# Two kinds of attention heads in turns, head by head, on one Trainium2 core

## Chip, cores and metric

The kernel runs on one core of one Trainium2 chip. The metric is the device time of one execution in microseconds (us); lower is better. Three runs of the kernel before took 2731.16, 2734.02 and 2737.94 us, a median of 2734.02 us.

## The reference, cut to what matters

One layer of an encoder for 2048 tokens of width 1024, all in float32: an adaLN-modulated RMS norm, a mixer with 16 heads of width 64, an output projection with a residual, a second norm, and a squared-ReLU MLP of width 4096. Eight heads are stick-breaking attention (called SB here) over all earlier keys:

```python
z = jnp.einsum('bqhd,bkhd->bhqk', qb, kb).astype(jnp.float32) * scale
log_beta = jax.nn.log_sigmoid(z)
log_1m_beta = jnp.where(strict, jax.nn.log_sigmoid(-z), 0.0)
suffix = lax.cumsum(log_1m_beta, axis=3, reverse=True) - log_1m_beta
w = jnp.where(strict, jnp.exp(log_beta + suffix), 0.0)
outs.append(jnp.einsum('bhqk,bkhd->bqhd', w.astype(v.dtype), vb))
```

The other eight are softmax attention over the query's own chunk of 64 keys and the eight chunks before it, with a learned bias (called CA here):

```python
s = jnp.einsum('bnqhd,bnkhd->bnhqk', qc, k_band).astype(jnp.float32) * (d ** -0.5)
s = s + bias[None, None]
p = jax.nn.softmax(s, axis=-1)
out = jnp.einsum('bnhqk,bnkhd->bnqhd', p.astype(v.dtype), v_band)
```

The heads' outputs stand side by side, SB first, and go through the output projection together. No head needs another head's result.

## The kernel before, in words

The program has three stages. The first makes the adaLN columns, the first norm and most of the input projection. The second, from about 457 us to 1408 us, is the attention. The third is the output projection of the last group of tokens and the MLP; it is almost all matrix products.

Tokens stand in reversed order, so "earlier keys" have higher indices, in four groups g of 512 tokens. Each float32 product is made of products of high and low halves in a reduced format; that is why operands come in pairs (`wth` and `wtl`, made by `split`: ScalarE copies the high part, VectorE subtracts to get the low part).

The attention's work is a list of **units** (L926 to L929), taken in order. An SB unit is one head, one group g of queries and one block c of 512 keys, c from g to 3; a CA unit is one head and one group of queries with its whole band of up to 1024 keys. There are 80 SB units (8, 16, 24 and 32 in groups 3, 2, 1, 0) and 32 CA units. Each unit is four **steps** of 128 queries. In the loop over steps (L992) the step at the front computes scores and weights, and the step LAG = 8 behind it (two units) turns its weights round and multiplies them with the values. In the program's order one pass does this:

```python
for j in js:
    back.transposes(j)      # PE, into PSUM tile wt
if front is not None:
    front.soft1(fs)         # SB: ACT sigmoids, DVE scan, POOL product; CA: DVE sum and minimum
while first:
    first.pop(0)()          # CA, the step before: DVE reciprocal, POOL product
for j in js:
    back.parts(j)           # ACT wth, DVE wtl
if front is not None:
    front.soft2(fs)         # CA: ACT Exp
...
if i + 1 < len(steps):
    u, st = steps[i + 1]
    u.scores(st)            # PE, into PSUM tile z or cz
fill(front.weight if front else 0.6)
```

`Ordered` (L42) keeps TensorE (PE), ScalarE (ACT), VectorE (DVE) and GpSimd (POOL) in exactly this order, so nearly every instruction of the stage has line L42 in the profile and is told apart by its tile. An SB step (`soft1`, L680) has two Sigmoid activations, tiles `b` and `z`; a CA step (`soft2`, L770) has one Exp activation, tile `e`. Sigmoid and Exp are in different function tables of ScalarE: where one follows the other, the compiled program holds an ACT_TABLE_LOAD.

The tiles `z`, `cz`, `ct` and `wt` share four PSUM buffers (`ppz`, L554). A step of an SB unit takes two of them, `z` for its scores and `wt` for one block of its transposes; a step whose back is a CA unit of groups 0 to 2 takes two `wt`, as such a unit has eight blocks in four steps.

Loads of a unit (q, k, and the bias of CA, L560 to L576 and L716) are issued by SP two units ahead, its values (L578) two steps into the unit. SP works its DMA queue in order. The bias has two buffers, CA's values two, most others three.

`fill` (L938) puts matrix products of other work between the steps, so that PE always has something: the rest of the input projection (`pf`) and the output projection of finished groups (`po`). How much it puts into a step goes by the step's weight (1.0 for SB, 0.7 on the diagonal, 0.9 or 0.495 for CA) over the weight that is left; what does not fit is done at the end.

When a unit closes a head, `finish` (L587) folds the sums into half of a tile `o`; two heads share one `o`. `keep` (L599) then splits it into `os` (one buffer) and stores it.

Of the kernel before, what the change touches and what calls it, by code (L numbers as in the profile page):

```python
# [9 lines left out]
F32 = mybir.dt.float32  # L10
# [8 lines left out]
P = 128  # L19
# [3 lines left out]
NH = 8  # L23
DFF = 4096
KT = D // P
TB = 512
NTB = S // TB
# [40 lines left out]
def encoder_kernel(ctx, tc, xT, c, g1, g2, w_in, gqk, bias, w_o, w1, w2, w_ada, b_ada, out):  # L68
# [472 lines left out]
    with ExitStack() as ph:  # L541
# [6 lines left out]
        op = ph.enter_context(tc.tile_pool(name="op", bufs=2))  # L548
# [38 lines left out]
        def finish(u):  # L587
            r = (u.h % 2) * HD
            q = HD - r
            if u.h % 2 == 0:  # L590
                pend["o"] = op.tile([P, TB], F32, tag="o", name=f"o{u.nm}")
            o = pend["o"]
            tmp = op.tile([P, TB], F32, tag="otmp", name=f"otmp{u.nm}")
            act.copy(tmp[r : r + HD, :], u.acc[q : q + HD, :])
            dve.tensor_tensor(o[r : r + HD, :], u.acc[r : r + HD, :], tmp[r : r + HD, :], op=ALU.add)
            if u.h % 2:
                soon.append(lambda: keep(u, o))

        def keep(u, o):  # L599

            os = op.tile([P, 2, TB], F32R, tag="os", name=f"os{u.nm}", bufs=1)
            split(os[:, 0, :], os[:, 1, :], o, pool)
            sp.dma_start(scr_m[u.g, u.ca * 4 + u.h // 2], os.bitcast(F32))
            if u.ca and u.h == NH - 1 and u.g > 0:
                filler.append(Filler(outproj, u.g))

        pend = {}

        class Unit:
# [26 lines left out]
            def values(self, j):  # L636
                if j == 0 and self.first:
                    pend["acc"] = ppo.tile([P, TB], F32, tag="acc", name=f"acc{self.nm}")
                self.acc = pend["acc"]
                wh, wl, cols, kb = self.wt.pop(j)  # L640
                end = self.last and j == len(self.blocks) - 1
                pe.matmul(self.acc[:, cols], self.v[:, kb, :], wh[:, cols], start=self.first and j == 0, stop=False)
                pe.matmul(self.acc[:, cols], self.v[:, kb, :], wl[:, cols], start=False, stop=end)
                if end:
                    soon.append(lambda: finish(self))
# [279 lines left out]
        CAP = 5  # L925
        units = []  # L926
        for g in range(NTB - 1, -1, -1):
            units += [SB(h, g, c) for h in range(NH) for c in range(g, NTB)]
            units += [CA(h, g) for h in range(NH)]  # L929
        have = set()  # L930
        filler = [Filler(fill_qkv, 1, hts[1], (2, 3, 0, 1, 10, 11)), Filler(fill_qkv, 0, None, (2, 3, 0, 1, 4, 5, 10, 11))]
        work = 14 * 48.0 + 5 * KT * KT * 3 / 2
# [59 lines left out]
        for i in range(len(steps) + LAG):  # L992
# [29 lines left out]
            if i + 1 < len(steps):  # L1022
                u, st = steps[i + 1]
# [398 lines left out]
```

## Time and profile before

| | us |
|---|---|
| median of three runs | 2734.02 |
| the profiled execution | 2737.44 |
| its span, first to last instruction | 2735.7 |
| PE busy in the span | 2625.1 (96%) |
| VectorE busy | 1929.8 (71%) |
| ScalarE busy | 1528.5 (56%) |
| GpSimd busy | 1023.8 (37%) |

The span is cut into 40 slices of 68 us; slices 7 to 20, counted from 0, hold the attention. A busy digit is a share in tenths. The PE's busy time includes matrix products that are pipelined and whose ends are modelled. Idle time of an engine is put down to the semaphore that came last, written "<-" with the engine and tile that released it.

### The profile page before, as it was taken

How to read it: one execution, taken by the hardware profiler on the slowest of the kernel's cores; microseconds unless marked ns; L12 is line 12 of the kernel's file. 1: busy time of each engine (PE TensorE's matmuls, PEld its weight loads, DVE VectorE, ACT ScalarE, POOL GpSimd, SP SyncE). 2: the span in 40 equal slices, each digit the busy share in tenths (PEclk: the TensorE clock that was granted, in tenths of full speed). 3: DMA queues.
4: the chain of work that ended last, by engine and by line, in shares of the span. 5: the costliest groups of instructions: out<-in, count | busy, mean ns of one | idle time of the engine just before them, and what ended most of it. 6: DMA issues, size and time to landing. Idle time of an engine off the chain costs nothing.

```text
span 2735.7 us, 42897 instructions
## 1 busy us (share of the span) xinstructions
PE 2625.1 (96%) x14192; PEld 2235.5 (82%) x14192; DVE 1929.8 (71%) x3329; ACT 1528.5 (56%) x2926; POOL 1023.8 (37%) x1116
## 2 busy tenths in 40 slices
PE   6998999899999999999988999999999999999999
PEld 5898998678778987878876888888878888888887
DVE  7565575788789988989747887765597655555564
ACT  5422433788678878878634455454465454544443
POOL 5342454566466656767524332100022422100000
PEclk9999999999999999999998999999999999999999
DMA  8978885987888688766777887785576444555574
GB/s 327 337 273 320 288 295 190 275 261 240 276 245 257 199 249 272 231 212 194 205 252 272 280 284 256 271 298 191 191 254 243 158 148 148 177 197 199 189 258 142
DMA packets 311197, 653.52 MB, mean 239 GB/s; under 512 B 29376, under 2 KB 118464, under 8 KB 301888
## 3 DMA queue, kind: packets, MB, share of 16 engines
q1 hardware_dynamic: 310336, 649.22, 70.7%
q8 instruction: 112, 1.84, 0.3%
q10 hardware_dynamic: 640, 1.57, 0.2%
q14 instruction: 109, 0.89, 0.1%
HBM read 459.31 MB, written 191.37 MB: 238 GB/s over the span
## 4 chain that ended last, share of the span: by engine, by line
PE 52%; DVE 2%; DMA 1%; ACT 1%; issue 1%; POOL 0%; SPq 0%; DVEq 0%; ACTq 0%
PE ps L42 44%; PE po L42 3%; PE acc L42 2%; PE wt L42 2%; PE z L42 1%; DVE h L129 1%; DVE ty L1063 1%; PE cz L42 0%; DMA wo<-scr_wo 0%; DMA ty<-scr_x 0%; DMA out_dram<-tx 0%; DVE tx L1301 0%; DVE p L42 0%; POOL ty L1106 0%; ACT ty L1107 0%
## 5 line engine op out<-in xcount | busy, mean ns | idle before, releaser
L42 PE MATMUL ps<-h,opw 128*128 128x512 f32 x2688 | 613.4, 391 | 6.7 <-ACT opw L128 4.0
L42 PE MATMUL ps<-oph,opv 128*128 128x512 f32 x2688 | 614.9, 391 | 4.1 <-DVE opv L129 3.5
L42 PEld LDWEIGHTS ps<-h,opw 128*128 128x128 f32 x2688 | 506.6, 189 | 113.3 <-ACT opw L128 4.5
L42 PEld LDWEIGHTS ps<-oph,opv 128*128 128x128 f32 x2688 | 506.4, 189 | 110.8 <-DVE opv L129 4.2
L42 POOL TENSOR_TENSOR b<-b,p 128x512 f32<-128x512 f32 (+1 forms) x320 | 359.6, 1124 | 197.0 <-DVE p L42 174.9
L42 DVE TENSOR_TENSOR wtl<-wt,wth 128x512 fp32r<-128x512 f32 (+3 forms) x544 | 290.4, 545 | 49.7 <-ACT wth L42 47.2
L42 ACT CAST wth<-wt 128x512 fp32r<-128x512 f32 (+3 forms) x544 | 257.5, 484 | 116.0 <-PE wt L42 99.9
L42 PE MATMUL pt<-wh,ht 128*128 128x256 f32 x1664 | 307.4, 286 | 7.9 <-DVE ht L129 5.8
L129 DVE TENSOR_TENSOR oph<-hr,oph 128x512 fp32r<-128x512 f32 x224 | 156.0, 697 | 208.0 <-ACT oph L128 207.8
L128 ACT CAST oph<-hr 128x512 fp32r<-128x512 f32 x224 | 139.4, 622 | 291.4 <-PE ps L42 286.4
L42 PEld LDWEIGHTS pt<-wh,ht 128*128 128x128 f32 x1664 | 263.1, 193 | 9.1 <-DVE ht L129 6.2
L42 DVE TENSOR_TENSOR_SCAN p<-z,p,zero 128x512 f32<-128x512 f32 x192 | 246.0, 1281 | 33.6 <-ACT z L42 28.7
L42 PE MATMUL pt<-wl,ht 128*128 128x256 f32 x832 | 236.5, 284 | 0.0
L42 PE MATMUL acc<-wth,v 128*128 128x512 f32 (+3 forms) x544 | 221.7, 412 | 3.1 <-DMA v<-scr_v 3.1
L42 ACT ACTIVATE b<-z 128x512 f32<-128x512 f32 (+1 forms) x320 | 171.4, 536 | 66.7 <-PE z L42 50.7
L42 PE MATMUL z<-k,q 128*128 128x512 f32 (+3 forms) x640 | 187.7, 375 | 14.0 <-DVE p L42 5.9
L42 POOL TENSOR_TENSOR e<-e,cols 128x640 f32<-128x640 f32 (+4 forms) x128 | 143.0, 1120 | 147.5 <-DVE cols L42 81.6
L42 PE MATMUL acc<-wtl,v 128*128 128x512 f32 (+3 forms) x544 | 186.3, 349 | 0.0
L42 PE MATMUL wt<-ident,b 128*128 128x128 f32 x1088 | 172.5, 274 | 6.6 <-DVE cols L42 4.9
L42 ACT ACTIVATE z<-z 128x512 f32<-128x512 f32 (+1 forms) x320 | 170.6, 533 | 0.0
L42 PEld LDWEIGHTS wt<-ident,b 128*128 128x128 f32 x1088 | 133.9, 141 | 37.5 <-DVE cols L42 6.9
L42 PE MATMUL po<-fx,ow 128*128 128x512 f32 x576 | 162.5, 397 | 0.0
(207 smaller groups left out, 4536.7 us busy)
## 6 DMA issues: line engine op xcount, KB each, us to landing
hr<-scr_hid SPq DMA_DIRECT2D x112, 512.0 KB, 3.5
v<-scr_v SPq DMA_DIRECT2D x136, 256.0 KB, 4.3
k<-scr_k SPq DMA_DIRECT2D x268, 128.0 KB, 4.1
w<-in_w_dram SPq DMA_DIRECT2D x64, 512.0 KB, 4.2
wr<-scr_s SPq DMA_DIRECT2D x64, 512.0 KB, 4.1
q<-scr_q SPq DMA_DIRECT2D x124, 256.0 KB, 5.3
fw<-scr_w SPq DMA_DIRECT2D x28, 1024.0 KB, 6.4
wa<-in_w_ada_dram SPq DMA_DIRECT2D x48, 512.0 KB, 6.4
```

Source lines behind the costliest of these rows:

```text
L42: return lambda *x, **y: self.tc.keep_in_program_order(f(*x, **y))
L128: act.copy(hi, src)
L129: (lo_eng or dve).tensor_tensor(lo, src, hi.bitcast(F32), op=ALU.subtract)
L1063: eng.tensor_tensor(out, a, b, op=op)
```

## The change

```diff
@@ finish
             if u.h % 2 == 0:
-                pend["o"] = op.tile([P, TB], F32, tag="o", name=f"o{u.nm}")
-            o = pend["o"]
+                pend["o", u.ca] = op.tile([P, TB], F32, tag="o", name=f"o{u.nm}", bufs=3)
+            o = pend["o", u.ca]
@@ the list of units
         for g in range(NTB - 1, -1, -1):
-            units += [SB(h, g, c) for h in range(NH) for c in range(g, NTB)]
-            units += [CA(h, g) for h in range(NH)]
+            for h in range(NH):
+                units += [SB(h, g, c) for c in range(g, NTB)]
+                units.append(CA(h, g))
```

Within a group the order was SB head 0 to 7, then CA head 0 to 7. Now SB head 0 is followed by CA head 0, then SB head 1, CA head 1, and so on. As two heads of each kind are now open at once, each kind has a tile `o` of its own, and `o` has three buffers and not two. All units, their steps and their matrix products stay the same in kind and number.

## The prediction, as put on record

> **What bounds the kernel now.** I read the page's busy times, its slices and the first line of its chain.
>
> ```profile
> PE 2625.1 (96%) x14192; PEld 2235.5 (82%) x14192; DVE 1929.8 (71%) x3329; ACT 1528.5 (56%) x2926; POOL 1023.8 (37%) x1116
> ...
> ACT  5422433788678878878634455454465454544443
> ...
> PE 52%; DVE 2%; DMA 1%; ACT 1%; issue 1%; POOL 0%; SPq 0%; DVEq 0%; ACTq 0%
> ```
>
> PE is busy 96% of the span and is by far the largest part of the chain. So an edit that leaves the matrix products as they are can only move PE's waits. ScalarE's 56% hides that its digits are 6 to 8 in the attention (slices 7 to 20); elsewhere it idles.
>
> Next the busy time by stretch. In each group the first row is the SB part and the second the CA part.
>
> ```profile
> 457.00:507.00 50.00, 48.54 (x265) 37.74 (x266) 37.53 (x62) 37.43 (x96) 32.32 (x61) 0.90 0.83 237
> 507.00:565.00 58.00, 46.29 (x261) 37.46 (x259) 38.14 (x139) 40.20 (x112) 28.93 (x40) 0.94 0.91 261
> 565.00:685.00 120.00, 116.22 (x756) 100.66 (x755) 105.89 (x146) 100.45 (x214) 82.77 (x134) 1.00 0.81 249
> 685.00:772.00 87.00, 79.99 (x463) 67.27 (x462) 62.29 (x220) 56.80 (x130) 42.81 (x36) 0.94 0.86 268
> 772.00:965.00 193.00, 189.39 (x1194) 163.39 (x1194) 171.23 (x226) 158.31 (x328) 129.82 (x197) 0.99 0.75 233
> 965.00:1046.00 81.00, 78.45 (x514) 69.15 (x513) 64.24 (x223) 57.36 (x132) 42.95 (x36) 1.00 0.87 265
> 1046.00:1305.00 259.00, 252.58 (x1407) 206.78 (x1405) 233.75 (x304) 213.09 (x426) 192.33 (x275) 1.00 0.70 221
> 1305.00:1408.00 103.00, 99.18 (x599) 84.26 (x598) 77.86 (x258) 66.64 (x152) 50.32 (x42) 1.00 0.67 201
> ```
>
> The columns after the length are PE, weight load, DVE, ACT and POOL busy, granted clock, DMA share and GB/s. Over the eight rows PE is busy 910.6 of 951 us. It is idle 40.4 us here, and that is nearly all that mixing the heads could win. Two CA parts stand out, those of groups 3 and 2: idle 11.7 of 58 us and 7.0 of 87, both at clock 0.94. The two later CA parts are idle 2.6 of 81 and 3.8 of 103. In the SB parts DVE is close behind PE (233.75 of 259.00, 90%) and ACT not far (82%).
>
> **What the change removes.** The CA parts end as such, and with them the rush of their loads. The waits of PE and of SP's queue in the attention:
>
> ```profile
> PE cz L42 <- DMA k<-scr_k: 4.7, 4, 1.8
> PE pf L42 <- DMA fw<-scr_w: 4.5, 2, 2.9
> PE acc L42 <- DMA v<-scr_v: 3.1, 1, 3.1
> ...
> SPq L721 <- DVE cols L42: 27.8, 17, 3.3
> ```
>
> PE waits 12.3 us for these loads, and SP's queue stands 27.8 us, with all later loads behind it, until one of the two bias buffers is free. With one or more SB units between two CA units the bias and value buffers are long free when they are wanted. If the parts of groups 3 and 2 idled only like the CA part of group 1 (2.55 of 81 us, 3.1%), that gave 11.7 + 7.0 - 0.031 x 145 = 14.2 us; a full clock over the same 145 us gave 6% of it, 8.7 us. So at most 22.9 us. I take half, **11 us**: loads' bytes stay the same, the DMA share of group 3 is 0.83 and 0.91 in its two parts, so the mean does not fall, and the refilling of the input projection (`fw`) meets some heads' loads in either order. Bounds 0 and 22.9.
>
> **What it adds: table loads.** Before, ScalarE goes from Sigmoid to Exp once in each group and back once, except at the end. Now it does so for each head. The compiled order of ScalarE's instructions shows 64 table loads in place of 8; the rest has the same kinds and numbers.
>
> ```profile
> L42 ACT ACT_TABLE_LOAD x7 | 9.0, 1283 | 1.2 <-PE z L42 0.7 <-DVE cols L42 0.4
> ```
>
> One load takes 1283 ns, so 56 more are 71.8 us of ScalarE, 14 loads or 18 us in each group. ScalarE's busy time then is 95.6 of 108 us in group 3 (77.63 + 18 by the rows above) and 297.7 of 362 in group 0: 89% and 82%. It does not become the bound by throughput. What counts is where a load stands in the order. The 1.2 us of idle time ahead of the seven, released by `z` and `cols`, says that a load waits for the data of the activation behind it, so it mostly comes after the data and not ahead of them.
>
> **SB to CA.** Three switches of before, with what PE waited behind them:
>
> ```profile
> 687.20 1.28 ACT L42 ACT_TABLE_LOAD   x1
> 688.49 0.83 ACT L42 ACTIVATE e<-s,cols 128x640 f32<-128x640 f32 x1
> 690.42 0.73 PE L42 MATMUL cz<-k,q 128*128 128x512 f32 x2 [0.34 <-DVE wtl L42]
> ...
> 971.64 0.73 PE L42 MATMUL cz<-k,q 128*128 128x512 f32 x2 [0.48 <-DVE wtl L42]
> ...
> 1309.41 0.66 PE L42 MATMUL wt<-ident,b 128*128 128x128 f32 x4 [0.55 <-DVE cols L42]
> ...
> 1310.76 0.73 PE L42 MATMUL cz<-k,q 128*128 128x512 f32 x2 [0.23 <-DVE wtl L42]
> ```
>
> Behind the load in ScalarE's queue stand `e` and then the next `wth`; DVE's `wtl` waits for that, and PE waits for the PSUM buffer that `wtl` frees. Price: 0.34, 0.48 and 0.78 us, mean 0.53. The weights `e` themselves are wanted eight steps later, which hides them. I take **0.5 us** for each of 28 more: 14 us.
>
> **CA to SB.** Here the load stands ahead of both sigmoids, and the scan of DVE, which frees `z`, behind them.
>
> ```profile
> 569.17 0.50 PE L42 MATMUL z<-k,q 128*128 128x256 f32 x2 [1.20 <-DVE cols L42]
> ...
> 779.08 1.08 PE L42 MATMUL wt<-ident,e 128*128 128x128 f32 x5 [2.74 <-DVE cols L42]
> ...
> 1046.16 0.68 PE L42 MATMUL z<-k,q 128*128 128x512 f32 x2
> 1048.18 1.28 ACT L42 ACT_TABLE_LOAD   x1
> 1049.48 0.60 ACT L42 ACTIVATE b<-z 128x512 f32<-128x512 f32 x1
> 1050.59 1.22 DVE L42 TENSOR_TENSOR_SCAN p<-z,zero 128x512 f32<-128x512 f32 x1 [2.84 <-ACT z L42]
> 1051.87 1.08 PE L42 MATMUL wt<-ident,e 128*128 128x128 f32 x5 [1.81 <-DVE cols L42]
> ```
>
> The scores lay ready from about 1046.9 us; ScalarE finished the last `e`, loaded for 1.28 us, did both sigmoids, DVE scanned until 1051.81, and at 1051.87 PE had its buffer. PE stood 1.20, 2.74 and 1.81 us at the three switches. In the two longer cases a CA unit of eight blocks was at the back: two `wt` and one `z` a step use four buffers up after a step and a third. In the new order the unit two places behind the first SB unit of a head is the SB unit ahead of the CA unit (in group 3 too, where every unit takes one `wt` a step), so PE can do one more round of transposes and value products before it stops, 1.1 us by the rows at 1309.41 and 1310.76 (1310.76 - 0.23 - 1309.41). That makes 1.81 - 1.1 = 0.7, and the case that already has one `wt` a step, at 569.17, shows 1.2. I take **1.0 us**, nearest to those two: 28 us for 28 more.
>
> The Trainium skill speaks against this change: "ScalarE: Activation LUTs", section "Rules for kernel authors", has functions grouped by table set, all of one done before the switch. Its section "What ACT_TABLE_LOAD costs" gives 1283 ns, as the trace does, and a drain of 1380 ns more; the trace shows no drain, as `e` starts at 688.49, when the load that began at 687.20 ends.
>
> **What it moves.** CA's values now go to PE while SB units are at the front, and the reverse; the sums of each engine stay. In the SB parts PE idles 1.5 + 3.8 + 3.6 + 6.4 = 15.3 us, mostly for a DVE that is 90% busy; with CA in between, DVE's share is even (233.75 + 77.86 of 362 us, 86%). That can win some of it back. I take nothing, as SB units still follow each other in groups 0 to 2 and the new stalls eat DVE's slack too; bounds 0 and 8 us.
>
> **What costs nothing, and its cover.** The `os` tile has one buffer, and now two `os` follow one unit apart.
>
> ```profile
> scr_m<-os SPq DMA_DIRECT2D x32, 512.0 KB, 3.2
> PE z L42 <- DVE st L198: 5.4, 1, 5.4
> ```
>
> A store lands in 3.2 us; with the split ahead of it that still fits in a unit of 58/8 = 7 us, the shortest. Were it late, ScalarE would wait in four pairs of group 3, up to 4 us in all. The second row is the start of the stage: PE waits 5.4 us for the last tiles of the stage before. The first CA unit's k tile is now loaded there, in a buffer that overlaps those tiles; it is wanted four steps later, which hides it, and without that cover it costs up to another 5 us. The fill's weights sum to the same, so the work left for the end does not change, and the end of the list is the same CA unit.
>
> **Sum.** 14 + 28 - 11 = +31 us. Against the profiled execution's own 2737.4 us that is 2768; the median of the three runs is 2734.0, 3.4 us lower, so I say **2765 us**.
>
> **The rivals.**
>
> *A, the smoothing wins (faster).* The loads fall into time in which ScalarE waits anyway:
>
> ```profile
> ACT wth L42 <- PE wt L42: 99.9, 146, 7.0
> ```
>
> That is 99.9 us of waiting for PE ahead of this one tile, against 71.8 of loads. If ScalarE reaches a load 1.28 us ahead of its data, the load is free. The deciding point: at a switch ScalarE must have been idle that long before, and the load must not wait for its data. Then only 0.3 us a pair is left, 28 x 0.3 = 8, against the full 22.9: 2734 - 15 = 2719 us. For it: the idle parts of groups 3 and 2. Against it: PE waits behind all six switches shown, and the loads wait for data.
>
> *B, switches cost what they did.* 28 x (0.53 + 1.92) = 69 us, with 1.92 the mean of 1.20, 2.74 and 1.81. And the longest of these waits also cost clock:
>
> ```profile
> 778.00:782.00 4.00, 2.82 (x14) 2.25 (x15) 3.91 (x7) 2.90 (x8) 2.75 (x4) 0.85 0.98 296
> 782.00:786.00 4.00, 4.00 (x22) 3.47 (x20) 2.66 (x5) 2.08 (x7) 1.86 (x4) 0.73 0.74 198
> ```
>
> 0.15 x 4 + 0.27 x 4 = 1.7 us of clock; at one switch in three that is 16 us more. With 69, 16 and no more than 5 won, 2734 + 80 = 2814 us. For it: it is the plain mean of rows. Against it: two of its three rows had the eight-block unit at the back.
>
> *C, both small.* The loads are half hidden (about 15 us) and the smoothing gives 15: 2734 us, within 0.3%, which is 8 us and about what a measurement of this kernel can tell from no change.
>
> *D, a switch takes twice the row's load.* Then ScalarE has 144 us more, 36 in group 3 (113.6 of 108 us: it becomes the bound), and each switch is 1.28 us dearer: 2765 + 28 x 2 x 1.28 = 2837 us. The skill's drain, in "What ACT_TABLE_LOAD costs", would make it so; the row at 688.49 speaks against it.
>
> That the heads do not alternate is no rival: the compiled order of each engine shows them in turns.
>
> **How the numbers follow.** The forecast, with its own range 2743 to 2790, has a chance of 0.55; A 0.13; B 0.20; C 0.09; D 0.03. Faster by over 0.3%: 0.13 (A). Within: 0.09 (C). Slower: 0.78. The range reaches into A and to B's sum, **2720 to 2815**, and leaves out D, the better half of A and the worse tail of B, some 0.15.
>
> **What the profile of after would show.** 64 table loads of about 1.28 us and ScalarE at about 1600 us busy. Right: PE's idle time in the attention some 70 us, in waits of 0.3 to 1.5 us for `wtl`, `p` and `cols` just behind loads; waits for `scr_k`, `scr_v`, `scr_w` well under 12.3 us, and SP's wait for the bias gone. Wrong if PE hardly waits behind loads (A), if waits near 2 us with dips of clock follow most returns to SB (B), or if the loss sits in the first and last 20 us of the stage.

## The result, and the profile after

| | before | after |
|---|---|---|
| median, five runs of each (us) | 2737.31 (2731.16 to 2738.68) | 2803.60 (2800.86 to 2804.67) |
| ratio, 95% interval | | 1.0238 (1.0224 to 1.0252) |
| the profiled execution | 2737.44 | 2804.67 |

The change costs 66.3 us. The direction is that of the forecast and the time lies in its range, but the loss is more than twice the 31 us of the sum.

First two of the same lines of the page, now of after: the busy times and ScalarE's slices.

```profile
PE 2641.4 (94%) x14192; PEld 2239.1 (80%) x14192; DVE 1928.9 (69%) x3329; ACT 1592.3 (57%) x2982; POOL 1026.4 (37%) x1116
...
ACT  5423433887878877878862444554455445544443
```

The matrix products are the same 14192. ScalarE is busy 1592.3 us against 1528.5, with 56 more instructions, and its slices 7 to 19 stand at 7 and 8 throughout, slice 20 at 6. The loads themselves, from the costliest groups:

```profile
L42 ACT ACT_TABLE_LOAD x64 | 82.1, 1283 | 4.0 <-DVE cols L42 2.5 <-PEq L1411 0.7
```

64 of them, 1283 ns each as before.

Next the busy time by group. The boundaries are the first score product of each group and, at the end, of the last CA unit, so that both fences cover nearly the same work (that of after has 24 matrix products more); the columns are those of the windows above. Before:

```profile
457.20:564.60 107.40, 94.45 (x522) 74.92 (x523) 75.28 (x199) 77.51 (x208) 60.85 (x99) 0.92 0.87 249
564.60:771.90 207.30, 196.49 (x1217) 168.11 (x1217) 168.42 (x365) 157.28 (x345) 125.97 (x169) 0.98 0.83 257
771.90:1046.20 274.30, 268.14 (x1710) 232.84 (x1709) 235.67 (x448) 215.98 (x460) 172.77 (x232) 0.99 0.79 243
1046.20:1379.60 333.40, 323.21 (x1833) 266.65 (x1831) 292.19 (x509) 261.72 (x538) 231.35 (x307) 1.00 0.70 219
457.20:1379.60 922.40, 882.29 (x5276) 742.52 (x5276) 771.56 (x1520) 712.48 (x1547) 590.95 (x806) 0.98 0.78 238
```

After:

```profile
461.10:583.60 122.50, 95.86 (x523) 76.46 (x524) 75.97 (x196) 93.88 (x217) 59.29 (x98) 0.91 0.76 222
583.60:809.90 226.30, 203.76 (x1230) 173.18 (x1229) 170.00 (x376) 175.75 (x368) 125.78 (x170) 0.97 0.81 246
809.90:1100.00 290.10, 269.72 (x1711) 231.75 (x1710) 234.74 (x451) 232.18 (x475) 173.20 (x233) 1.00 0.74 229
1100.00:1451.30 351.30, 330.83 (x1842) 268.02 (x1841) 292.04 (x511) 278.30 (x557) 233.61 (x310) 0.99 0.66 205
461.10:1451.30 990.20, 900.17 (x5300) 749.42 (x5301) 772.75 (x1532) 780.11 (x1614) 591.88 (x808) 0.98 0.73 223
```

Each group is longer by about as much: 15.1, 19.0, 15.8 and 17.9 us, 67.8 in all. A group has 8 heads and so 14 loads more, whatever its length; a loss that goes with the number of switches and not with the work looks like this. PE's idle time rises from 40.1 (922.40 - 882.29) to 90.0 us; the other 17.9 us are busy time. The 24 products are some of it; but over the whole program, with the same 14192 products, PE is busy 16.3 us longer (2641.4 against 2625.1). The stage also begins 3.9 us later.

The waits of the attention, after, with the total, the times and the longest:

```profile
ACT wth L42 <- PE wt L42: 115.2, 129, 6.0
...
PE z L42 <- DVE cols L42: 45.5, 31, 3.1
...
PE cz L42 <- DVE wtl L42: 9.1, 13, 1.3
...
PE cz L42 <- DMA k<-scr_k: 5.9, 1, 5.9
```

There are 31 returns from CA to SB, and 30 of them show a wait of the third score product `z` for `cols`, the reciprocal that DVE makes just behind the scan: 44.8 us of the 45.5, 1.49 us each. (The 31st wait of the row, 0.75 us, stands ahead of a first score product.) The way to CA shows in 13 waits for `wtl`, at most 1.3 us. ScalarE still idles 115.2 us for PE ahead of `wth`, so it has time for the loads, only not at the places where they stand. One return in the timeline of after (group 0), the lines of PE, ScalarE and DVE that matter:

```profile
1143.50 0.63 PE L42 MATMUL z<-k,q 128*128 128x512 f32 x2
1143.77 0.83 ACT L42 ACTIVATE e<-s,cols 128x640 f32<-128x640 f32 x1
...
1144.01 0.94 PE L42 MATMUL po<-fx,ow 128*128 128x512 f32 x3
...
1144.70 1.28 ACT L42 ACT_TABLE_LOAD   x1
...
1145.99 0.60 ACT L42 ACTIVATE b<-z 128x512 f32<-128x512 f32 x1
...
1147.17 1.23 DVE L42 TENSOR_TENSOR_SCAN p<-z,zero 128x512 f32<-128x512 f32 x1 [2.57 <-ACT z L42]
...
1148.45 0.50 PE L42 MATMUL z<-k,q 128*128 128x256 f32 x2 [1.27 <-DVE cols L42]
```

PE has the scores ready at 1144.1; then the load, two sigmoids and the scan pass one after the other, and at the third `z` PE stands 1.27 us. That is the place the prediction named. The returns are not alike: the 16 behind CA units of groups 3 and 2 stop PE for 1.91 us on average, the 15 behind those of groups 1 and 0 for 0.94. At 15 of the 16 a copy `otmp` of 0.58 us, part of closing a head, stands on ScalarE ahead of the load; at the 15 others it does not.

### The profile page after: what moved, and what is told of

It reads as the page before. It is cut to its first block, busy times and chain, and to the rows that moved or that the text cites. A ratio compares the mean times of both kernels' runs of the same rounds, so it can differ in the third digit from the quotient of the medians.

```text
span 2802.8 us, 42713 instructions
## 1 busy us (share of the span) xinstructions
PE 2641.4 (94%) x14192; PEld 2239.1 (80%) x14192; DVE 1928.9 (69%) x3329; ACT 1592.3 (57%) x2982; POOL 1026.4 (37%) x1116
## 3 DMA queue, kind: packets, MB, share of 16 engines
q8 instruction: 112, 1.84, 0.3%
## 4 chain that ended last, share of the span: by engine, by line
PE 42%; DVE 4%; DMA 2%; issue 1%; POOL 1%; ACT 1%; SPq 0%; DVEq 0%; POOLq 0%; ACTq 0%
PE ps L42 39%; PE po L42 1%; DVE h L129 1%; DMA ty<-scr_x 1%; DMA wo<-scr_wo 1%; DVE ty L1064 1%; PE acc L42 0%; DMA w2s<-in_w_dram 0%; PE wt L42 0%; POOL ty L1107 0%; DVE opv L129 0%; DMA out_dram<-tx 0%; PE pso L42 0%; DVE opw L129 0%; DVE p L42 0%
## 5 line engine op out<-in xcount | busy, mean ns | idle before, releaser
L42 ACT CAST wth<-wt 128x512 fp32r<-128x512 f32 (+3 forms) x544 | 257.1, 484 | 120.7 <-PE wt L42 115.2
L42 PE MATMUL z<-k,q 128*128 128x512 f32 (+3 forms) x640 | 192.8, 384 | 62.5 <-DVE cols L42 45.5
L42 PEld LDWEIGHTS z<-k,q 128*128 128x128 f32 x640 | 112.8, 194 | 90.9 <-DVE cols L42 55.9
```

Source lines behind the costliest of these rows:

```text
L42: return lambda *x, **y: self.tc.keep_in_program_order(f(*x, **y))
```

## The experiments

The table gives each median less the median of before that was measured together with it, since that one lay between 2736.1 and 2739.3 us. Its uncertainty is that of the ratio, some 3 to 5 us.

| kernel | median | less before | ratio, 95% interval |
|---|---|---|---|
| one_table_turns | 2741.88 | +5.8 | 1.0019 (1.0009 to 1.0029) |
| one_table_eights | 2726.30 | -9.8 | 0.9963 (0.9949 to 0.9976) |
| by_two | 2744.78 | +8.7 | 1.0033 (1.0020 to 1.0046) |
| one_table_by_two | 2720.43 | -17.7 | 0.9934 (0.9916 to 0.9951) |
| o_alone | 2735.28 | -0.8 | 0.9998 (0.9986 to 1.0009) |
| stop_to_ca | 2769.89 | +31.8 | 1.0111 (1.0092 to 1.0129) |
| stop_to_sb | 2801.89 | +63.8 | 1.0235 (1.0217 to 1.0253) |
| short_stop_to_ca | 2756.18 | +16.9 | 1.0061 (1.0045 to 1.0078) |
| short_stop_to_sb | 2775.98 | +36.7 | 1.0134 (1.0116 to 1.0152) |
| one_table_start | 2735.68 | -2.4 | 0.9994 (0.9984 to 1.0005) |
| finish_later | 2830.14 | +90.9 | 1.0336 (1.0318 to 1.0354) |
| no_sum_turns | 2726.87 | -10.3 | 0.9966 (0.9955 to 0.9978) |
| no_sum_eights | 2715.23 | -22.0 | 0.9918 (0.9901 to 0.9935) |
| fill_by_back | 2745.98 | +7.1 | 1.0029 (1.0020 to 1.0039) |
| one_table_start_later | 2754.71 | +15.8 | 1.0062 (1.0042 to 1.0083) |
| tanh_by_two | 2726.26 | -13.0 | 0.9947 (0.9930 to 0.9963) |
| tanh_eights | 2734.73 | -2.5 | 0.9988 (0.9978 to 0.9998) |
| onesig_by_two | 2722.68 | -14.5 | 0.9947 (0.9930 to 0.9964) |

**The loads and the mixing apart.** In the changed kernel and in the one before, CA's function is put into the table of SB's, and nothing else moves. The weights become other numbers, and `e` takes as long as before (97.9 us in all against 97.8):

```diff
-    act.activation(e[:, :n], self.s[:, :n], AF.Exp, bias=self.m, scale=-1.0, accum_out=l)
+    act.activation(e[:, :n], self.s[:, :n], AF.Sigmoid, bias=self.m, scale=-1.0, accum_out=l)
```

> The changed order, with Sigmoid in the place of Exp in the softmax heads (their weights are other numbers; the instructions, their sizes and order stay): one function table serves the whole attention, so the 63 loads in it go. Theory T, the loads' 1.28 us reach PE nearly whole and the smoothing wins some 10 to 20 us: 2715 to 2735 us, PE's waits for the scan behind a CA unit gone. Rival R, the loads are mostly hidden and the mixing itself costs (CA blocks behind SB units fill PSUM and load VectorE): 2775 us or more.

> The old order with the same Sigmoid in place of Exp: 7 loads fewer. T: 7 to 15 us faster than before, 2722 to 2730 us. R: 2735 us, nothing to see. It also says whether the other function by itself changes anything.

Without the loads the new order costs 5.8 us in place of 66.3: the loads are 60.5 of it, 0.96 us for each of 63. In the old order seven loads cost 9.8 us, 1.4 each. So 56 more loads cost 50.7 us. The rest is the surprise: mixing alone is 15.6 us slower (5.8 + 9.8; by the two intervals, give or take 5), not faster. one_table_turns lies between its two expectations, one_table_eights within that of theory T. The waits of PE in the attention of one_table_turns show what a switch is without its load, and what has become of the waits for loads from memory:

```profile
PE z L42 <- DVE p L42: 8.5, 13, 3.2
PE z L42 <- DVE cols L42: 6.8, 15, 1.4
PE cz L42 <- DMA k<-scr_k: 5.9, 1, 5.9
...
PE pf L42 <- DMA fw<-scr_w: 4.8, 1, 4.8
PE wt L42 <- DVE p L42: 4.3, 11, 0.8
PE z L42 <- DMA k<-scr_k: 3.4, 1, 3.4
PE ct L42 <- DVE p L42: 2.9, 3, 2.4
PE cz L42 <- DVE p L42: 2.7, 7, 0.6
```

`z` waits 6.8 us for `cols` where it waited 45.5. The loads from memory cost PE 14.1 us (5.9 + 4.8 + 3.4) against 10.5 in one_table_eights; without the 5.9 for the first CA unit's `k` they are 8.2. `cols` as a whole is down from 12.2 to 7.6. But PE waits 18.4 us for `p`, the tile of the scans. In one_table_eights that is 7.0:

```profile
PE z L42 <- DVE p L42: 5.9, 10, 2.2
...
PE wt L42 <- DVE p L42: 0.9, 2, 0.5
...
PE ct L42 <- DVE p L42: 0.2, 1, 0.2
```

**The tile `o` alone.** The two lines of the diff in `finish`, in the old order.

> The old order with only the tile part of the change: an o tile for each kind and three buffers, which moves the pools behind it by 2 KB. T and R: as before, 2737 us within 4. A third theory, that the moved tiles make loads at the stage's ends wait: 2742 us or more.

No difference: 0.9998, with 1 inside the interval. The tile has no part in the result.

**Half the switches.** Two SB heads, then two CA heads:

```diff
-            for h in range(NH):
-                units += [SB(h, g, c) for c in range(g, NTB)]
-                units.append(CA(h, g))
+            for h0 in range(0, NH, 2):
+                hs = range(h0, h0 + 2)
+                units += [SB(h, g, c) for h in hs for c in range(g, NTB)]
+                units += [CA(h, g) for h in hs]
```

> Two SB heads, then the same two CA heads: 32 loads in all, 24 more than before and 32 fewer than head by head. T: the loss goes with the loads, 24 of 56 of 66 us, about 2765 us. R: the CA units still come behind SB units in the four pairs of each group, 2785 us or more.

> Two and two, with Sigmoid for Exp, so without loads. If the 31 loads of that order cost 1 us each, as the 63 do head by head: 2714 us, and mixing by two wins 12 us over eight and eight without loads (2726.3). If those loads are cheap (0.4 us), 2732 us, and mixing wins nothing in this form either.

by_two came 20 us below the lower expectation. Its loads (32 in the program) cost 26.4 us (8.7 + 17.7), 0.85 each, good to 0.2 by the intervals and so no different from turns. Without loads two by two is 7.9 us faster than eight by eight (give or take 6), where one by one is 15.6 slower; its 2720 us lies between the two expectations, nearer to the first. So an order that mixes can win, but not the one that was asked about; that the win is the smoothing which the prediction had in mind was not tried. The timeline of a return to SB in by_two, group 0 again, with an eight-block CA unit at the back:

```profile
1223.01 0.63 PE L42 MATMUL z<-k,q 128*128 128x512 f32 x2
...
1223.52 0.93 PE L42 MATMUL po<-fx,ow 128*128 128x512 f32 x3
...
1224.20 1.28 ACT L42 ACT_TABLE_LOAD   x1
...
1226.47 0.71 PE L42 MATMUL po<-fx,ow 128*128 128x512 f32 x2
...
1226.62 1.23 DVE L42 TENSOR_TENSOR_SCAN p<-z,zero 128x512 f32<-128x512 f32 x1 [2.51 <-ACT z L42]
...
1227.90 0.55 PE L42 MATMUL wt<-ident,e 128*128 128x128 f32 x3 [0.71 <-DVE cols L42]
```

The scan ends as long after the first `z` as in after: 4.84 us (1226.62 + 1.23 - 1223.01) against 4.90. PE does eight transposes and four value products ahead of its stop in either kernel, here in one step, there in two. But here five filling products `po` come ahead of the stop, there three: PE stops 4.2 us after that `z` (1227.90 - 0.71 - 1223.01) and not 3.7, and waits 0.71 and not 1.27 us. Eight of the 15 returns in groups 1 and 0 of after reach their stop as late, after 4.19 to 4.23 us, and are as short, 0.72 to 0.79 us:

```profile
1099.92 0.62 PE L42 MATMUL z<-k,q 128*128 128x512 f32 x2
...
1104.88 0.50 PE L42 MATMUL z<-k,q 128*128 128x256 f32 x2 [0.77 <-DVE cols L42]
```

So these returns show no difference by the unit at the back. What differs is the filling products ahead of the stop and how late ScalarE comes to the load.

**A plain stop in place of the load.** To price the two directions apart, one_table_turns gets copies on ScalarE at one kind of switch, into a tile that nobody reads, where the load would stand:

```diff
+                if 0 < i < len(steps) and (kinds[i - 1], kinds[i]) == (1, 0):
+                    for _ in range(6):
+                        act.copy(idle[:, :140], zero.to_broadcast([P, 140]))
                 front.soft1(fs)
```

`kinds` holds 0 for a step of SB and 1 for one of CA. For the way to CA the pair is (0, 1) and the copies stand ahead of `soft2`; the short stops have four copies.

> The changed order with Sigmoid for Exp (no loads, 2741.9 us), and about 1.28 us of ScalarE copies into a scratch tile put where the load ahead of the first softmax step of a head stood, 32 of them. The prediction's price, 0.5 us each: 2758 us. Theory P, the return to SB carries nearly all: under 2752 us. Rival Q, both switches cost alike, 1 us each: 2773 us.

> The same copies where the load ahead of the first sigmoids of a head stood, 31 of them. The prediction's price, 1.0 us each: 2773 us. P: 2785 us or more. Q: 2773 us.

The copies came out longer than meant, so these two price a stop of 6 x 0.306 = 1.84 us. The group of copies, and PE's wait behind them, of stop_to_sb:

```profile
L42 ACT CAST idle<-zero 128x140 bf16<-128x140 f32 x186 | 56.9, 306 | 5.0
```

```profile
PE z L42 <- DVE cols L42: 59.5, 32, 3.3
```

And PE's wait of stop_to_ca, for the other direction:

```profile
PE cz L42 <- DVE wtl L42: 15.3, 20, 1.5
```

The same two waits as in after, each with its own kind of switch. Over one_table_turns the stops cost 26.0 us for 32 on the way to CA (0.81 each) and 58.0 for 31 on the way back (1.87 each). So the return carries more, but not nearly all (theory P), and the two are not alike (rival Q). The short ones, 4 x 0.306 = 1.22 us:

> As stop_to_ca, which added 28 us to 2741.9 with stops that came out at 1.85 us (six copies of 308 ns each); now four copies, 1.23 us, close to one load. If the price is in proportion to the stop: 18 us more, 2760 us. If ScalarE's slack hides the first part of a stop: under 2754 us. The prediction's 0.5 us each: 2758 us.

> As stop_to_sb (60 us more with 1.85 us), now 1.23 us. In proportion: 40 us more, 2782 us. Slack hides the first part: under 2773 us, which is the prediction's 1.0 us each. With short_stop_to_ca it should add up to the 62 us that the loads of the changed kernel cost.

11.1 us or 0.35 each, and 30.9 us or 1.0 each. By the intervals each price is good to about 0.17; both times lie between the expectation of proportion and that of hidden slack. From there on a return costs at least its full length: 0.62 us more of stop is 0.87 us more of time. Together the short stops make 42.0 us, where the loads make 60.5. Most of that gap is that the copies were the shorter stop. They overlap the instruction before and the one behind by some 0.1 us each, and a load does not. From the end of ScalarE's instruction before the switch to the start of the one behind it, the load takes 1.31 us on the way back and 1.39 on the way to CA, the four copies 1.17 and 1.13, the six 1.85 and 1.80 (means over the timelines, the first switch to CA left out). At one and the same return (at 1099.92 us in after) the scan ends 3.49 us after the first score begins without any stop, 4.71 with four copies, 4.91 with the load. Between the short and the long stops a load's length makes 1.18 us for a return and 0.53 for a way to CA, 53 us in all. The other 7 us lie within the uncertainty of about 8; and that the two kinds of stop, run apart, simply add up was not tried. The prediction read in the row of the seven loads that a load waits for the data of the activation behind it. That happens, but it is small: all idle time ahead of the 64 loads of after is the 4.0 us of their row, 2.5 of it for `cols` on the way to CA.

**Two SB heads at the start.** In one_table_turns the second and third unit change places, so that the first CA unit comes one later:

```diff
+        units[1], units[2] = units[2], units[1]
```

> The changed order without loads, but at the very start the first two SB heads come ahead of the first CA head, so that the first CA unit's keys are not wanted while the last stores of the stage before are under way. If the start is what the mixing itself loses: 2735 us, some 6 less than 2741.9. If the loss is spread over the groups: 2740 us or more.

One exchange at the very start wins 8.2 us by the table (6.2 by the two medians of the kernels). PE's wait of 5.9 us for the first CA unit's `k` has gone. Why there was one can be read in SP's queue in the timeline of after:

```profile
459.74 1.65 SPq L200 DMA_DIRECT2D scr_k<-st  x2
...
464.41 1.09 SPq L564 DMA_DIRECT2D q<-scr_q  x2
465.68 1.10 SPq L572 DMA_DIRECT2D k<-scr_k  x2
```

The loads of the first CA unit stand behind the last stores of the stage before, and PE wants this `k` at about 464.5 us (470.44 less its wait of 5.93); ahead of its `q` the queue also stands 2.5 us for the first score products of PE. That the unit comes four steps into the stage was not time enough. What is left is 7 to 9 us of the mixing. Groups 2 and 0 of one_table_start:

```profile
558.10:768.40 210.30, 198.88 (x1229) 169.65 (x1228) 169.97 (x377) 154.94 (x352) 125.99 (x170) 0.98 0.86 258
...
1040.20:1381.10 340.90, 328.37 (x1842) 268.80 (x1840) 292.09 (x512) 259.10 (x542) 233.38 (x310) 0.99 0.69 214
```

And of one_table_eights:

```profile
559.70:763.60 203.90, 195.12 (x1216) 167.51 (x1217) 168.11 (x365) 155.09 (x343) 126.13 (x169) 0.98 0.84 260
...
1033.70:1366.80 333.10, 324.51 (x1832) 267.76 (x1831) 292.11 (x509) 259.30 (x535) 231.76 (x307) 0.99 0.71 219
```

Groups 2 and 0 lose 6.4 and 7.8 us in turns; group 1 loses 1.7 and group 3 wins 3.3. (These two profiled executions are 12.2 us apart, the medians 9.4.) DVE, ACT and POOL do the same work in both, and the clock is the same. PE's idle time grows by 2.6 and 3.9 us in the two groups: its waits for the scans' tile `p` go from 5.4 to 15.9 us, those for `cols` from 7.1 to 3.3. The rest is busy time, with 22 products more in the two windows. So PE meets late scans more often in turns; three attempts to find out why follow.

**The jobs that close a head.** In the timeline of group 2 the copy `otmp` and the sum `o` of the head just closed stand inside a return to SB:

```profile
668.81 0.58 ACT L42 COPY otmp<-acc 64x512 f32<-64x512 f32 x1
...
669.41 1.28 ACT L42 ACT_TABLE_LOAD   x1
669.42 0.69 DVE L42 TENSOR_TENSOR o<-acc,otmp 64x512 f32<-64x512 f32 x1 [1.29 <-ACT otmp L42]
```

The copy holds the load up by 0.6 us. In groups 1 and 0 it stands elsewhere. finish_later puts them two steps later, in the changed kernel:

```diff
-                    soon.append(lambda: finish(self))
+                    later.add(3, lambda: soon.append(lambda: finish(self)))
```

> The changed kernel with its loads, but the jobs that close a head (ScalarE's copy otmp and VectorE's sum o) come two steps later, so that in groups 3 and 2 they no longer stand at the return to SB, between the last Exp and the load. Theory F, this coincidence makes these groups' switches dearer: 2790 to 2798 us, the gain in groups 3 and 2. Rival, order of small jobs does not matter: 2803 us.

24.6 us slower than after, so the forecast of this run was wrong. The waits of PE in the attention of finish_later:

```profile
PE z L42 <- DVE cols L42: 35.5, 28, 2.5
PE wt L42 <- DVE cols L42: 19.9, 17, 1.9
...
PE acc L42 <- DVE o L42: 6.8, 7, 1.5
```

The returns do get cheaper (35.5 us against 45.5), but new waits of `wt` and `acc` come up (`wt` waited 3.4 us for `cols` in after): the loss has moved to other steps, and PE now waits for the sum before it may use the PSUM tile `acc` again.

> The kernel of one_table_start with the jobs that close a head (the sums of its parts, the split of the outputs, the store) two steps later, as in finish_later but with no table loads in the attention. Theory X: in turns these jobs meet the first steps of the unit after next, of the other kind, and that meeting is what the 9.4 us of mixing are; then about 2728. Theory W: not so; 2735 to 2740, or slower, as the jobs only meet other steps.

Without loads the same move costs 18.2 us. So it is not a price of the loads, and the jobs stand better where they were than two steps later. no_sum takes VectorE's sum out of them:

```diff
-            tmp = op.tile([P, TB], F32, tag="otmp", name=f"otmp{u.nm}")
-            act.copy(tmp[r : r + HD, :], u.acc[q : q + HD, :])
-            dve.tensor_tensor(o[r : r + HD, :], u.acc[r : r + HD, :], tmp[r : r + HD, :], op=ALU.add)
+            act.copy(o[r : r + HD, :], u.acc[q : q + HD, :])
```

> one_table_start (head by head, no loads, the first two SB heads ahead; 2735.7 us), with VectorE's sum at the end of a head left out: the output takes one of its two halves alone. That is 64 x 0.69 = 44 us less of VectorE. Theory V, head by head VectorE is full in some SB units and PE waits for its scans: 2726 us or less. Rival W, the 9 us that mixing costs is not VectorE's: 2732 us or more.

> The same sum left out of one_table_eights (2726.3 us). V: 3 us less, 2723 us, so that the gap to no_sum_turns shrinks to some 3 us. W: the gap of 9 us stays, whatever both win.

The sum costs 7.9 us in turns and 12.2 in eights; the gap between the orders does not shrink to theory V's 3 us (11.7 us against 7.4 before, give or take 6). no_sum_turns alone came near theory V's number, but no_sum_eights won even more. So the sum is ruled out as the cause of the gap.

**The filling products.** Dealt by the unit at the back as well:

```diff
+            if front.g == 3:
+                return front.weight
+            if front.ca:
+                return 1.05
+            return 0.6 if front.diag else 0.5 if back.ca else 1.3
...
-            fill(front.weight if front else 0.6)
+            fill(share(front, back))
```

> The kernel of one_table_start (heads in turns, one function table, two SB heads first) with the filling products dealt by the unit at the back as well as by the one at the front: a step with a CA unit behind an SB unit gets 0.5, an SB step with SB behind it 1.3 (0.6 on the diagonal), a CA step 1.05; group 3 as before. What is filled over the whole stage stays the same. Theory V: the 9.4 us of mixing that are left come because a unit's fill is set by its front alone, so that steps with eight blocks of CA values behind are too full for PE and the other SB steps are bound by VectorE; then the time falls from 2735.7 to about 2727, with group 2 at about 205 us and group 0 at about 334. Theory W: they do not depend on the fill; 2735 to 2737, groups as in one_table_start (210.4 and 340.9 us).

9.5 us slower than one_table_start. That is neither theory's number; theory V falls, at least with these shares. Why PE waits longer for scans in groups 2 and 0, and with it the cause of the last 7 to 9 us, stays open.

**Other ways to the same weights.** SB's weights can also be had as differences of the running product that the scan makes, so that one sigmoid is enough; and that sigmoid can be a tanh, with a copy that halves it and adds a half:

```diff
-                act.activation(b[:, :n], z[:, :n], AF.Sigmoid, scale=0.125)
-                act.activation(z[:, :n], z[:, :n], AF.Sigmoid, scale=-0.125)
+                act.activation(z[:, :n], z[:, :n], AF.Tanh, scale=-0.0625)
+                act.activation(z[:, :n], z[:, :n], AF.Copy, scale=0.5, bias=0.5)
...
-                pool.tensor_tensor(b[:, :n], b[:, :n], pt[:, :n], op=ALU.mult)
+                pool.tensor_tensor(b[:, :n], pt[:, :n], pt[:, 1 : n + 1], op=ALU.subtract)
```

onesig_by_two keeps one Sigmoid of scale -0.125 in place of the two new lines. Both stand in the order of by_two, tanh_eights in the old one.

> A version that computes the reference: two heads of a kind in turn, SB weights as differences of the running product, its factors from Tanh, which stands in one function table with Exp, and an affine Copy; two activations a step as before, no loads in the attention. If all that counts is loads and order: 2720 us as one_table_by_two, faster than both kernels. If GpSimd's or ScalarE's new forms are dearer: 2735 us or more.

> The version with Tanh and differences, no loads, in the old order of eight and eight. If the order by two is worth the 6 us that the one-table kernels showed (2720.4 against 2726.3): 2732 us against the 2726.3 of tanh_by_two. If nothing of it is left: 2726 us.

> Two by two with the loads, but one sigmoid a step in place of two (SB weights as differences of the running product): 320 activations or 171 us less of ScalarE, 32 loads stay. If a load costs because the chain load, two sigmoids, scan is long: the price falls from 0.8 to 0.4 us a load, 2725 to 2733 us. If the load alone sets the price: 2744 us, as by_two.

With Tanh the program holds no load in the attention, and two by two at 2726.26 us beats the kernel before by 0.53% (0.37 to 0.70); in the old order the same edit wins 2.5 us, so some 10 of the 13 come from the order. tanh_by_two lies between its two expectations. onesig_by_two keeps all 32 loads and is as fast, 2722.68, just below its lower expectation: against by_two the one sigmoid less on the chain behind each load, and in every step, is worth 23.2 us; how much of that is the loads' price was not separated. tanh_by_two and onesig_by_two, equal within their intervals, are the fastest that compute all of the reference, and both beat the kernel before and the one after.

## Why the prediction was right and wrong

**"What bounds the kernel now"** held in the main. 49.9 us of the 66.3 are idle time of PE in the attention. But PE is also busy 16.3 us longer over the whole program for the same products, which no term had. 12.7 of that go when the loads go (2628.7 in one_table_turns). The granted clock is a part of it at most: 0.984 over the whole of after and 0.986 of before are some 6 us, an estimate from these two. Outside the four groups, the stage begins 3.9 us later, and the part behind them is 4.6 us shorter, with 23 products fewer. One digit was misread: slice 20 of before, which holds the attention's end, is a 3 and not 6 to 8; no term rests on it.

**The mixing is the step that failed: "What the change removes", -11 us, with "What it moves" and the start put at nothing beside it.** The prediction has mixing as a gain of 11, with bounds of 0 and 22.9. Mixing without loads costs 15.6 us, 26.6 on the wrong side and outside these bounds. What was to go did go in part: SP's wait for the bias is gone from the waits of after, and without table loads PE's waits for loads from memory other than the first CA unit's `k` fall from 10.5 to 8.2 us, those for `cols` from 12.2 to 7.6. That is some 7 us of waits; the clock of groups 3 and 2, the other part of the 22.9, did not rise (0.91 and 0.98 in one_table_turns, 0.92 and 0.98 before). But that first `k` costs 5.9 us, PE's waits for scans grow from 7.0 to 18.4, and PE is busy 9.2 us longer for the same products (2628.7 against 2619.5 in one_table_eights). In after itself loads from memory hold PE for only 6.4 us, as the prediction said, while the table loads hold it too. The value 11 had no row for the new order behind it, only the idle time of the old one.

**"What costs nothing", the start.** Half of this was right: `o` costs nothing (o_alone), and `os` makes ScalarE wait once, for 4.8 us, behind the last unit of after, while PE has 22 us of filling products to do. The cover "four steps later" did not hold. The step was wrong by 6 to 8 us, just over its own bound of 5.

**"What it moves", 0 (bounds 0 to 8 won).** No gain; the 7 to 9 us lost in groups 2 and 0 lie outside the bounds, which excluded a loss. With the start they make up the 15.6. What came up are the longer waits of PE for scans; why they are longer is open.

**"What it adds", 42 us for 56 loads: the mechanism was right, its size somewhat too small.** They cost 50.7. The price of 0.5 us for a way to CA is that of a plain stop as long as the load (0.53), the price of 1.0 for a return a little less (1.18). The waits are where they were said to be: `z` for `cols` behind returns, `cz` for `wtl` on the way to CA. They were forecast at 0.3 to 1.5 us; the mean of a return is 1.49 and the longest 3.1.

The reason for the 1.0 does not hold, and that it came near is in part luck: it stands between two kinds of return, 1.91 us where closing a head holds ScalarE up ahead of the load, and 0.94 elsewhere. The prediction held the eight-block CA unit at the back to be what made two returns of before long, and an SB unit there to be milder, by one round of products. by_two has the CA unit there, and 11 such returns stop PE for 0.79 us on average. What the two long returns of before have is a late ScalarE: their loads begin 3.50 and 2.02 us after the first score product, that of by_two 1.19.

**The warning of the Trainium skill.** The rule of the Trainium skill cited from "ScalarE: Activation LUTs", section "Rules for kernel authors", to do all of one table set before the switch, agrees with the trace in its direction: each of the three orders was slower with loads than without them. It does not rank orders by itself: without loads two by two was faster than eight by eight. And onesig_by_two, with 32 loads, beats tanh_eights, which has none in the attention (2722.68 against 2734.73 us), though these two also differ by one activation a step. The drain that the Trainium skill gives in the section "What ACT_TABLE_LOAD costs" is still not to be seen: in after the load that begins at 1144.70 for 1.28 us is followed by `b` at 1145.99.

**The rivals.** B's time, 2814, is 10 us off, but not by its mechanism. It had the added switches at 69 us and 16 of clock; they cost 50.7, the clock bears some 6 of the 16, and the rest was mixing. Of B's sign, waits near 2 us with dips of the clock, there is some: eight of the 31 returns stop PE for 1.9 us or more, and the 4 us behind have a clock of 0.57 (from 497.60) or 0.72 (from 615.50), but also 1.00 (from 703.40). A's condition, that ScalarE has been idle ahead of each load, was met on average (115.2 us of waiting for PE) and not at the switches (4.0 us ahead of all 64 loads). C is ruled out by the size, D by the loads' length.

**The numbers.** Of the 35 us that the sum fell short, 26.6 are the mixing and 8.7 the loads' price, each good to about 5. The smoothing was bounded by 0 on the side of loss, with no row that excluded a loss; bounds as wide on that side as on the other, -23 to +23, would have held the 15.6.

## What to carry to other kernels

When work of two kinds is interleaved, price two things apart: what each switch puts on the chain that frees the bound engine's buffers, and what the new neighbourhood does without any switch cost; the second can have either sign, and one by one and two by two may differ by it. A table load costs by what stands ahead of it and behind it until the bound engine has its buffer, and by how much work that engine holds meanwhile: shorten that chain, or put more work beside it, before counting loads. An engine with more than 100 us of idle time can still be late at each of 31 places.

## What the runs showed that was not expected

A table load of 1.283 us holds ScalarE longer than four copies of 1.22 us in sum (1.31 against 1.17 us on the way back), as copies overlap their neighbours and the load does not; with that, most of what the loads cost more than the copies (60.5 against 42.0 us) is length. The price of a stop on the way back to SB is not in proportion to its length: 1.0 us for 1.22, 1.87 for 1.84, each good to 0.17. And PE's busy time for the same products rises where it is stopped often, 900.17 us against 885.99, with the same mean clock of 0.98 in both stretches; which of it is modelled ends of matmuls and which is real stays open.
